# The first phase of a transformer-layer kernel: loads, modulation and stream preparation rewritten in a fixed order

## The chip, the core and the metric

The kernel runs on one core of one Trainium2 chip. The metric is the device time of one execution in microseconds (us). The core's engines are TensorE (PE in the rows; PEld are its weight loads), VectorE (DVE), ScalarE (ACT), GpSimd (POOL) and SyncE (SP, which issues the weight DMAs). The measured time before is the median of three runs; the trace is of one further, profiled execution.

## The reference

One layer works on 256 latent tokens `x` and 256 context tokens `ctx`, each with 2048 channels:

```python
mod   = silu(c) @ w_mod + b_mod          # c: 2048 values; w_mod: 2048 x 12288
mod_c = silu(c_ctx) @ w_mod + b_mod
sa, ca, ga, sm, cm, gm = split(mod, 6)   # the context needs only sa_c, ca_c
h   = rmsnorm(x, nw) * (1 + ca) + sa
h_c = rmsnorm(ctx, nw) * (1 + ca_c) + sa_c
q, k, v from h @ w_in;  k_c, v_c from h_c @ w_in     # rmsnorm over heads, rope on q, k
mix = (sigmoid(g_a) * diff_attention(q, [k, k_c], [v, v_c]) @ w_a_up
     + sigmoid(g_b) * multiscale_pool(h @ w_p) @ w_b_up) @ w_o
x = x + ga * mix
x = x + gm * (relu(modulate(x, sm, cm) @ w_ff1) ** 2 @ w_ff2)
```

The change touches the part up to `h`, `h_c` and the first half of `q` and `k`.

## The kernel before

Every weight is streamed through SBUF in chunks of 512 KB (128 partitions x 1024 floats). `load_next` takes the next chunk of a planned list: SP issues its DMA into one of five `raw` buffers, ACT rounds it to a high half `whi` (L213), DVE subtracts to get the low half `wlo` (L214), and PE multiplies. A product of two floats is made of three products of halves (high x high, high x low, low x high), so a weight chunk of `w_q` or `w_k` with one stream of 256 tokens takes 12 matmuls (L241 to L243), and the chunk of a modulation weight takes four (L347: the two 512-column pieces of `whi` and of `wlo`, against `cv`, whose four columns are the halves of silu(c) and silu(c_ctx)). `whi` and `wlo` have three buffers each; `wchunk` loads two chunks ahead of the one that is used (AHEAD).

The time up to about 167 us is called the first phase here. Its steps in the program are:

- The squares of the x stream are summed (`square_sums`: ACT squares, L459; an add of two tiles, L460; PE sums over partitions with a matrix `mean`, L461) and `rsq` makes the inverse norm `rms[0]` of them.
- `w_m0`, the modulation weights of the first 256 channels, comes in two halves of four chunks, each split like all others.
- Seven stretches m = 1 to 7 follow. Each streams eight chunks of `w_m` (M0 to M7 below) into one PSUM bank, copies the four result rows to SBUF (`mod_rows`, ACT), turns them into columns with four transposes (`mod_columns`, L359, then small DVE operations L365 to L369), and makes with them two of the sixteen 128-channel pieces of the hidden stream of x (`hL`) and of the context (`hC`). `hidden` does that for each piece with a DVE operation that scales and norms (L380), an ACT operation that adds the bias and rounds (L381), and a DVE operation for the low half (L382).
- As soon as pieces exist, `first_steps` multiplies them with the first group of `w_k` for x ("kx"), of the kept `w_k` for the context ("kc"), and of `w_q` ("q"). The split of `w_k` is kept in the tile `first`.
- In stretch 2 the context's squares are summed, with the add of L460 on POOL; its inverse norm is `rms[1]`.

The order in which these instructions stand on each engine's queue is chosen by a scheduler, except for those wrapped in `pin`. The phase's loads all go through SP's queue in the order of the planned list `stream`.

After the phase, `qk_evac` norms and rotates q and k, with the last steps put off by a number of chunks (`later(wait, turn)`), and PE transposes them (`qkT`, L447). `pooling` forms sums over token windows by repeated adds on POOL (L744) and puts off `pool_diff` (edges and differences on DVE, L756 to L760) by three chunks. The two feed-forward products follow: 896 matmuls of 512 and 896 of 256 columns with `w_ff1` as the stationary operand (L939, L942), then `w_ff2`.

Of the kernel before, what the change touches and what calls it, by code (L numbers as in the profile page):

```python
# [17 lines left out]
P = 128  # L18
# [30 lines left out]
def layer(ctx: ExitStack, tc, a, out):  # L49
# [61 lines left out]
    def raw_chunk(src, n=1024):  # L111
        raw = pool.tile([P, n], F32, tag="raw", name="raw", bufs=5)
        nc.sync.dma_start(raw, src)
        return raw
# [9 lines left out]
    def plan(name, *idx, rate=0.0):  # L124
# [8 lines left out]
    for m in range(9):  # L133
        if m == 0:
            for half in range(2):
                for i in range(4):
                    plan("w_m0", half, i)
        for i in range(8 if m > 0 else 0):
            if m < 8:
                plan("w_m", m - 1, i)  # L140
            for at, n, j in carried[m]:
                if at == i and n != "kc":
                    plan("w_k" if n == "kx" else "w_q", 0, j)
            if m == 1 and i > 5 or m == 2 and i < 2:
                plan("cT", (8 * m + i - 14))
            if m == 3 and i == 4:
                plan("prq")
    for n, g, rate in (("w_v", 0, 1.5), ("w_q", 1, 1.0), ("w_k", 1, 1.5), ("w_v", 1, 1.5)):
# [37 lines left out]
    loaded = []  # L186
    done = [0]

    def load_next():
# [14 lines left out]
        raw = raw_chunk(src, n)  # L204
        if key[:2] == ("w_k", 0):
# [17 lines left out]
    def wchunk(*key, ahead=AHEAD):  # L223
        while len(loaded) < min(done[0] + 1 + ahead, len(stream)) or loaded[done[0]][1] is None:
            if loaded and done[0] < len(loaded) and loaded[done[0]][1] is None:
                done[0] += 1
                continue
            load_next()
        got, hi, lo = loaded[done[0]]
        assert got == key, (got, key)  # L230
        loaded[done[0]] = None
# [25 lines left out]

    prm = pool.tile([P, PRM_W], F32, tag="prm", name="prm")
    prq = s8("prq", [P, PRQ_W])
    nc.sync.dma_start(prm, a["prm"])  # L260
    xT = s16("xT", [P, KT, T])
    cT = s16("cT", [P, KT, T])
    for i in range(4):
        nc.sync.dma_start(xT[:, 4 * i:4 * i + 4, :], a["xT"][i])
# [12 lines left out]
    ebias = pool.tile([P, 1], F32, tag="ebias", name="ebias")  # L277
    vec.memset(ebias, -32.0 * math.log(2.0))
    epsb = pool.tile([P, 1], F32, tag="epsb", name="epsb")
# [7 lines left out]
    tc.keep_in_program_order(act.preload_act_table_set("natural_log_exp_and_others"))  # L287
    sil = pool.tile([P, 2, KT], F32, tag="sil", name="sil")
# [6 lines left out]
    b1 = small("b1", 16)  # L295
# [796 lines left out]
```

## Time and profile before

| | us |
|---|---|
| median of three runs | 1522.79 (1521.77 to 1524.62) |
| the profiled execution | 1519.78 |
| its span, first to last instruction | 1517.7 |
| PE busy | 1480.7 (98%) |
| DVE busy | 1063.2 (70%) |
| ACT busy | 755.7 (50%) |
| first DMA queue (weights) | 345.49 MB |

The busy time of PE is a sum of modelled, overlapping matmuls, so a share near 100% does not say that PE runs at its peak. The windows below cut the first phase where the last modulation matmul of a stretch stands: w_m0 ends at 25.8 us, stretch 1 at 43.6, stretch 2 at 72.1, stretch 3 at 89.1, and stretch 7 at 155.2. The profile's mean granted clock of PE is 0.994 of full speed over the span.

### The profile page before, as it was taken

Reading aid. Unit: us, or ns where it says so; the run is one execution under the profiler, and the core shown is the slowest. Engines: PE = TensorE matmul, PEld = TensorE weight load, DVE = VectorE, ACT = ScalarE, POOL = GpSimd, SP = SyncE. Lnnn points to the kernel's source line nnn. Section 1 sums busy time; section 2 is a strip of 40 time slices with the busy share of each in tenths; the row PEclk is TensorE's granted clock in tenths of the full one; section 3 lists DMA queues with packets and bytes.
Section 4 is the critical chain, followed back from the end, with each engine's and each line's share of the span. In section 5 each row is a group of like instructions: output and inputs, shape, how many; then the busy total and the mean of one; then the engine's idle time right before and its main releaser. Section 6 shows DMA issues by size and latency. Waiting matters only on the chain.

```text
span 1517.7 us, 19767 instructions
## 1 busy us (share of the span) xinstructions
PE 1480.7 (98%) x7336; PEld 1232.8 (81%) x7336; DVE 1063.2 (70%) x1280; ACT 755.7 (50%) x1007; POOL 129.3 (9%) x124
## 2 busy tenths in 40 slices
PE   7899999999989999999999999999999999999998
PEld 5677877768878888888879988888888888888887
DVE  7799878777887767666757665666666555555675
ACT  6677534556655444444444554544444454444432
POOL 0100111000140000000000100100000000000170
PEclk9899999999999999999999999999999999999999
DMA  8888668556568787788755677767777666666664
GB/s 314 310 283 308 214 215 285 177 167 193 167 216 300 254 275 272 242 295 296 235 181 168 220 251 245 232 217 244 231 241 240 202 188 193 193 187 193 184 200 142
DMA packets 97439, 347.82 MB, mean 229 GB/s; under 512 B 11072, under 2 KB 11712, under 8 KB 97344
## 3 DMA queue, kind: packets, MB, share of 16 engines
q1 hardware_dynamic: 96768, 345.49, 70.4%
q8 instruction: 57, 0.93, 0.3%
q0 software_dynamic: 576, 1.08, 0.2%
q14 instruction: 38, 0.31, 0.1%
HBM read 344.44 MB, written 2.10 MB: 228 GB/s over the span
## 4 chain that ended last, share of the span: by engine, by line
PE 88%; issue 3%; DVE 3%; DMA 3%; ACT 1%; POOL 1%; DVEq 0%; SPq 0%; ACTq 0%; POOLq 0%
PE f L939 14%; PE f L411 8%; PE f L410 8%; PE f L413 8%; PE f L942 7%; PE pg L413 4%; PE pg L410 4%; PE pg L411 4%; PE pyy L410 2%; PE wo L410 2%; PE wo L413 2%; PE wo L411 2%; PE pyy L413 2%; PE pyy L411 2%; PE v L411 2%
## 5 line engine op out<-in xcount | busy, mean ns | idle before, releaser
L214 DVE TENSOR_TENSOR wlo<-raw,whi 128x1024 fp32r<-128x1024 f32 x507 | 628.6, 1244 | 365.2 <-ACT whi L213 350.9
L213 ACT CAST whi<-raw 128x1024 fp32r<-128x1024 f32 x507 | 529.8, 1047 | 587.3 <-PE f L411 178.1
L939 PE MATMUL f<-h,whi 128*128 128x512 f32 x896 | 224.2, 392 | 0.0
L411 PE MATMUL f<-whi,act 128*128 128x512 f32 x512 | 199.3, 389 | 0.0
L410 PE MATMUL f<-whi,act 128*128 128x512 f32 x512 | 199.3, 389 | 0.0
L939 PEld LDWEIGHTS f<-h,whi 128*128 128x128 f32 x896 | 161.5, 189 | 29.1
L588 DVE SCALAR_TENSOR_TENSOR macc<-raw,sil,macc 128x1024 f32<-128x1024 f32 x128 | 166.2, 1299 | 1.4 <-DMA raw<-in_w_cm_dram 0.8
L413 PE MATMUL f<-wlo,act 128*128 128x512 f32 x512 | 136.8, 389 | 0.0
L942 PEld LDWEIGHTS f<-h,wlo 128*128 128x128 f32 x896 | 122.2, 190 | 8.7
L942 PE MATMUL f<-h,wlo 128*128 128x256 f32 x896 | 124.9, 282 | 0.0
L413 PEld LDWEIGHTS f<-wlo,act 128*128 128x128 f32 x512 | 96.1, 188 | 20.0
L411 PEld LDWEIGHTS f<-whi,act 128*128 128x128 f32 x512 | 96.1, 188 | 19.8
L410 PEld LDWEIGHTS f<-whi,act 128*128 128x128 f32 x512 | 96.1, 188 | 19.8
L410 PE MATMUL pg<-whi,hL 128*128 128x512 f32 x256 | 100.5, 393 | 0.0
L411 PE MATMUL pg<-whi,hL 128*128 128x512 f32 x256 | 99.7, 389 | 0.0
L950 POOL TENSOR_TENSOR rsq<-relu 128x512 f32<-128x512 f32 x28 | 29.2, 1042 | 537.6 <-ACT relu L949 516.7
L413 PE MATMUL pg<-wlo,hL 128*128 128x512 f32 x256 | 68.6, 390 | 2.5 <-DVE wlo L214 2.5
L413 PEld LDWEIGHTS pg<-wlo,hL 128*128 128x128 f32 x256 | 48.0, 188 | 12.9 <-DVE wlo L214 2.9
L410 PEld LDWEIGHTS pg<-whi,hL 128*128 128x128 f32 x256 | 48.1, 188 | 10.1 <-issue 0.2
L411 PEld LDWEIGHTS pg<-whi,hL 128*128 128x128 f32 x256 | 48.1, 188 | 10.1 <-issue 0.2
L410 PE MATMUL wo<-whi,mix 128*128 128x512 f32 x128 | 49.9, 390 | 0.0
L411 PE MATMUL wo<-whi,mix 128*128 128x512 f32 x128 | 49.8, 389 | 0.0
(267 smaller groups left out, 2205.1 us busy)
## 6 DMA issues: line engine op xcount, KB each, us to landing
raw<-in_w_ff_dram SPq DMA_DIRECT2D x240, 512.0 KB, 4.3
raw<-in_w_m_dram SPq DMA_DIRECT2D x64, 512.0 KB, 4.9
raw<-in_w_ga_dram SPq DMA_DIRECT2D x32, 512.0 KB, 4.6
raw<-in_w_cm_dram SPq DMA_DIRECT2D x32, 512.0 KB, 4.6
raw<-in_w_gb_in_dram SPq DMA_DIRECT2D x32, 512.0 KB, 4.5
raw<-in_w_ga_in_dram SPq DMA_DIRECT2D x32, 512.0 KB, 4.4
raw<-in_w_sm_dram SPq DMA_DIRECT2D x32, 512.0 KB, 4.7
raw<-in_w_o_dram SPq DMA_DIRECT2D x32, 512.0 KB, 4.6
```

What stands on the lines that cost most here:

```text
L213: act.copy(hi, raw)
L214: vec.tensor_sub(lo, raw, hi.bitcast(F32))
L410: pe.matmul(banks[t], tok(h, k, 0, tt), wt, start=k == 0, stop=False)
L411: pe.matmul(banks[t], tok(h, k, 1, tt), wt, start=False, stop=False)
L413: pe.matmul(banks[t], tok(h, k, 0, tt), wt, start=False, stop=k == 2 * nk - 1)
L588: pin(vec.scalar_tensor_tensor(acc, raw, sil[:, 0, k:k + 1], acc, ALU.mult, ALU.add))
L939: pe.matmul(ps, hi[:, kk * P:kk * P + P], both(h2, k), start=k == 0, stop=False)
L942: pe.matmul(ps[:, T:2 * T], lo[:, kk * P:kk * P + P], act_slice(h2, k, 0), start=False, stop=k == KT - 1)
L950: gp.tensor_mul(sq, r, r)
```

## The change

All instructions of PE, ACT, DVE and SP in the first phase are now pinned in program order (`ordered_all`), and the program itself is written as a table, `STRETCHES`, of the chunks of each stretch (M: modulation, C: a quarter of the context, K and Q: chunks of `w_k` and `w_q`, T: the rope tables), with a table `then` of what follows each of them. In rows of the changed kernel all such instructions carry line 67, the wrapper's.

- The four chunks of the first half of `w_m0` are loaded ahead of x. `w_m0` is no longer split: PE multiplies the raw floats against `sil`, the two columns silu(c) and silu(c_ctx), with 16 matmuls of 256 columns for each half.
- `hidden` takes streams that were normed before (`scale_stream`, one DVE multiplication for two pieces); ACT scales and adds the bias, rounds both pieces in one cast, and the low half of both is one DVE subtraction, issued behind the next chunk (`low_halves`).
- The context is loaded and squared in stretch 1, and its four adds are on DVE. The chunks of `w_q` come a stretch later than before, so that 60 matmuls of q and k are left behind the last stretch, where there were 48.
- The bias columns are added in one DVE operation instead of two.
- `whi` and `wlo` are placed as six fixed tiles of 1028 floats; the weights that are a stationary operand (`w_p`, `w_ff1a`, `w_ff1`) start 4 floats (16 bytes) into them.
- `qk_evac` waits one chunk longer, `late_split` too, and the `pool_diff` of the last window (g = 3) is put off by five chunks instead of three.

```diff
-            return (lambda *a, **k: pin(emit(*a, **k))) if ordered[0] else emit
-    act, vec = Engine(nc.scalar), Engine(nc.vector)
+            return (lambda *a, **k: pin(emit(*a, **k))) if any(f[0] for f in self.flags) else emit
+    act, vec = Engine(nc.scalar, ordered, ordered_all), Engine(nc.vector, ordered, ordered_all)
+    pe, sp = Engine(nc.tensor, ordered_all), Engine(nc.sync, ordered_all)
...
-    carried = {1: ((1, "kx", 0), (4, "q", 0)), 2: ((2, "kx", 1), (4, "q", 1)),
-               3: ((0, "kc", 0), (3, "kx", 2), (5, "q", 2), (6, "kc", 1))}
+    STRETCHES = [None,
+                 ("M0", "C0", "M1", "C1", "M2", "C2", "K0", "C3", "M3", "M4", "Q0", "M5", "M6", "M7"),
+                 ("M0", "M1", "M2", "M3", "K1", "M4", "M5", "Q1", "M6", "T0", "M7"),
+                 ("M0", "M1", "M2", "M3", "K2", "M4", "M5", "M6", "M7")]
     for m in range(4, 8):
-        carried[m] = ((0, "kc", m - 2), (2, "kx", m - 1), (4, "q", m - 1))
-    carried[8] = ((0, "kc", 6), (0, "kx", 7), (0, "q", 7), (0, "kc", 7))
+        STRETCHES.append(("M0", "M1", f"Q{m - 2}", "M2", "M3", "M4", f"K{m - 1}", "M5", "M6", "M7"))
+    STRETCHES.append(("Q6", "K7", "Q7"))
...
+    STATIONARY, OFFSET = ("w_p", "w_ff1a", "w_ff1"), 4
+    def halves(n, at):
+        i = chunks[0] % 3
+        chunks[0] += 1
+        return [pool.tile([P, 1028], F32R, tag=f"{part}{i}", name=part, bufs=1)[:, at:at + n] for part in ("whi", "wlo")]
...
+        if key[0] == "w_m0":
+            loaded.append((key, raw, raw))
+            return
...
-            hi = pool.tile([P, n], F32R, tag="whi", name="whi", bufs=3)
-            lo = pool.tile([P, n], F32R, tag="wlo", name="wlo", bufs=3)
+            hi, lo = halves(n, OFFSET if key[0] in STATIONARY else 0)
...
+    def mod_whole(half, i, ps, ahead):
+        raw, _ = wchunk("w_m0", half, i, ahead=ahead)
+        for kk in range(4):
+            k = 4 * i + kk
+            pe.matmul(ps[0:2, 0:256], sil[:, :, k], raw[:, kk * 256:kk * 256 + 256], start=k == 0, stop=k == 15)
...
+    def scale_stream(t, k):
+        src = (xT, cT)[t][:, k:k + 2, :]
+        vec.tensor_mul(src, src, rms[t].unsqueeze(1).broadcast_to([P, 2, T]))
...
         for kk in range(n):
-            ht, k8 = h[(k + kk) // 8], (k + kk) % 8
-            u = hw[:, kk, :]
-            bias = c3[:, n + kk, t:t + 1]
-            vec.scalar_tensor_tensor(u, src[:, k + kk, :], c3[:, kk, t:t + 1], rms[t], ALU.mult, ALU.mult)
-            act.activation(ht[:, 0, k8, :], u, AF.Identity, bias=bias)
-            vec.scalar_tensor_tensor(ht[:, 1, k8, :], u, bias, ht[:, 0, k8, :].bitcast(F32), ALU.add, ALU.subtract)
+            act.activation(hw[:, kk, :], src[:, k + kk, :], AF.Identity, bias=c3[:, n + kk, t:t + 1],
+                           scale=c3[:, kk, t:t + 1])
+        hi, lo = ht[:, 0, k8:k8 + n, :], ht[:, 1, k8:k8 + n, :]
+        act.copy(hi, hw)
+        lows.append(lambda: vec.tensor_sub(lo, hw, hi.bitcast(F32)))
...
+    ps = bank("mod")
     for i in range(4):
+        mod_whole(0, i, ps, ahead=3)
+        if i == 0:
+            for q in range(4):
+                sp.dma_start(xT[:, 4 * q:4 * q + 4, :], a["xT"][q])
...
+    for m in range(4, 8):
+        k = 2 * m - 2
+        then[m] = {"M0": [lambda: take_rows(before), partial(context_keys, m - 2), partial(aside, 1)],
+                   "M1": [partial(turn_rows, k), partial(aside, 1)],
+                   "M2": [partial(lambda k: hidden(k, 0, cols[k]), k), partial(aside, 1)],
+                   "M3": [partial(scale_stream, 1, k), partial(aside, 1)],
+                   "M5": [partial(lambda k: hidden(k, 1, cols[k]), k)]}
...
-        qk_evac(kb[t], t, 0, kT, 2, 2 + t)
+        qk_evac(kb[t], t, 0, kT, 2, 3 + t)
...
-            later(3, partial(pool_diff, g, w, ps, sums))
+            later(3 if g < 3 else 5, partial(pool_diff, g, w, ps, sums))
```

The first place is the start of PE's queue (`ssq` is the bank of x's squares, `mod` that of the modulation). Before it read:

```order
L461 MATMUL ssq<-sq,mean 128x256 x8
L347 MATMUL mod<-whi,cv 128x256 x4
L347 MATMUL mod<-wlo,cv 128x256 x4
L347 MATMUL mod<-whi,cv 128x256 x4
L347 MATMUL mod<-wlo,cv 128x256 x4
L347 MATMUL mod<-whi,cv 128x256 x4
```

and in the changed kernel it reads:

```order
L67 MATMUL mod<-raw,sil 2x256 x16
L67 MATMUL ssq<-sq,mean 128x256 x6
L67 MATMUL modT<-prm,rows 128x2 x2
L67 MATMUL ssq<-sq,mean 128x256 x2
L67 MATMUL mod<-raw,sil 2x256 x16
L67 MATMUL mod<-whi,cv 128x512 x2
```

The sums of x's squares moved behind a whole half of w_m0, and 64 matmuls on halves became 32 on raw floats.

The second place is DVE's queue at stretch 2 (`rq_t` and `aT` belong to the inverse norm, `col` to the modulation columns, `hw` to `hidden`). Before:

```order
L365 TENSOR_TENSOR col<-ms 128x8
L367 TENSOR_TENSOR col<-col,b_87 128x4
L369 TENSOR_TENSOR col<-col,prm 128x4
L368 TENSOR_TENSOR col<-col,prm 128x4
L380 SCALAR_TENSOR_TENSOR hw<-xT,col,aT 128x256 x2
L214 TENSOR_TENSOR wlo<-raw,whi 128x1024
L382 SCALAR_TENSOR_TENSOR hL_94<-hw,col,hL_94 128x256 x2
L214 TENSOR_TENSOR wlo<-raw,whi 128x1024
L214 TENSOR_TENSOR first<-raw,first 128x1024
L214 TENSOR_TENSOR wlo<-raw,whi 128x1024 x6
```

and in the changed kernel:

```order
L67 TENSOR_TENSOR wlo<-raw,whi 128x1024 x3
L67 TENSOR_TENSOR col<-ms 128x8
L67 TENSOR_TENSOR col<-col,prm 128x8
L67 TENSOR_TENSOR col<-col,prm 128x4
L67 TENSOR_TENSOR first<-raw,first 128x1024
L67 TENSOR_TENSOR cT<-cT,aT 128x512
L67 TENSOR_TENSOR wlo<-raw,whi 128x1024
L67 TENSOR_TENSOR hL_98<-hw,hL_98 128x512
L67 TENSOR_TENSOR xT<-xT,aT 128x512
L67 TENSOR_TENSOR wlo<-raw,whi 128x1024 x2
```

Four operations of `hidden` on 256 columns became one subtraction and one multiplication on 512, and a subtraction of weights stands between each of them and what it waits for.

The third place is DVE's queue at `pool_diff` of g = 2 (its end, the differences `d` and their low half `dl`) and g = 3 (its start, on the window sums `za` that POOL forms, L758). Before:

```order
L760 SCALAR_TENSOR_TENSOR d<-zb,pin 128x256
L214 TENSOR_TENSOR wlo<-raw,whi 128x1024
L238 TENSOR_TENSOR dl<-d,dh 128x512
L588 SCALAR_TENSOR_TENSOR macc<-raw,sil,macc 128x1024
L238 TENSOR_TENSOR yb<-py,yb 128x512
L758 TENSOR_TENSOR za<-za,prm 128x7 x2
L214 TENSOR_TENSOR wlo<-raw,whi 128x1024
```

and in the changed kernel (its L862 was L758, its L256 was L238):

```order
L864 SCALAR_TENSOR_TENSOR d<-zb,pin 128x256
L256 TENSOR_TENSOR dl<-d,dh 128x512
L692 SCALAR_TENSOR_TENSOR macc<-raw,sil,macc 128x1024
L231 TENSOR_TENSOR wlo<-raw,whi 128x1024
L256 TENSOR_TENSOR yb<-py,yb 128x512
L862 TENSOR_TENSOR za<-za,prm 128x7 x2
L231 TENSOR_TENSOR wlo<-raw,whi 128x1024
```

The two short multiplications stay ahead of the same subtraction of weights; one other subtraction moved from ahead of `dl` to behind it.

## Rows read from the trace of the kernel before

**Rows 1.** The page's busy times: busy us, share of the span, instructions.

```profile
PE 1480.7 (98%) x7336; PEld 1232.8 (81%) x7336; DVE 1063.2 (70%) x1280; ACT 755.7 (50%) x1007; POOL 129.3 (9%) x124
```

**Rows 2.** Windows: length, busy PE, PEld, DVE, ACT, POOL; clock, DMA share, GB/s.

```profile
0.00:25.80 25.80, 15.83 (x83) 12.60 (x84) 17.28 (x31) 18.20 (x26) 1.82 (x6) 1.00 0.90 317
25.80:43.60 17.80, 15.26 (x59) 9.69 (x57) 12.82 (x16) 9.90 (x12) 0.00 (x0) 1.00 0.92 342
43.60:72.10 28.50, 25.09 (x90) 18.04 (x90) 23.86 (x28) 21.64 (x31) 7.23 (x4) 0.82 0.82 281
72.10:89.10 17.00, 17.00 (x77) 13.48 (x75) 16.61 (x34) 12.03 (x17) 0.00 (x0) 1.00 0.81 262
...
155.20:171.00 15.80, 15.17 (x70) 12.26 (x69) 11.85 (x27) 9.24 (x16) 0.42 (x1) 1.00 0.60 228
```

**Rows 3.** Windows: stretches 4 to 7 together, the fastest loads, the slow clock.

```profile
89.10:155.20 66.10, 65.05 (x285) 50.47 (x285) 60.72 (x99) 47.90 (x63) 0.00 (x0) 1.00 0.87 304
...
38.00:43.00 5.00, 3.81 (x15) 2.03 (x14) 2.45 (x2) 2.04 (x2) 0.00 (x0) 1.00 1.03 416
43.00:53.00 10.00, 7.46 (x19) 3.93 (x19) 6.83 (x11) 7.66 (x13) 2.80 (x2) 0.62 0.91 347
```

**Rows 4.** DVE groups by shape, 0 to 171 us: busy us, mean ns, idle before.

```profile
L214 DVE TENSOR_TENSOR wlo<-raw,whi 128x1024 fp32r<-128x1024 f32 x75 | 93.1, 1259 | 16.9 <-ACT whi L213 16.4
L382 DVE SCALAR_TENSOR_TENSOR hL<-hw,col,hL 128x256 fp32r<-128x256 f32 x16 | 8.1, 541 | 0.0
L380 DVE SCALAR_TENSOR_TENSOR hw<-cT,col,aT 128x256 f32<-128x256 f32 x16 | 7.2, 476 | 0.0
L460 DVE TENSOR_TENSOR sq<-sq 128x512 f32<-128x512 f32 x4 | 2.8, 692 | 4.3 <-ACT sq L459 4.3
L318 DVE TENSOR_TENSOR tabs<-prq 128x32 f32<-128x32 f32 x8 | 1.1, 183 | 0.0
```

**Rows 5.** ACT groups by shape, 0 to 171 us, same columns.

```profile
L213 ACT CAST whi<-raw 128x1024 fp32r<-128x1024 f32 x75 | 77.7, 1047 | 29.2 <-DVE wlo L214 8.4 <-DMA raw<-in_w_m_dram 7.3 <-PE mod L347 5.8
L381 ACT ACTIVATE hL<-hw,col 128x256 fp32r<-128x256 f32 x16 | 7.4, 502 | 6.4 <-DVE hw L380 6.2
L459 ACT ACTIVATE sq<-cT 128x512 f32<-128x512 f32 x8 | 4.7, 622 | 0.0
```

**Rows 6.** Timeline of PE in the first feed-forward product: start, length, count.

```profile
1115.77 1.98 PE L939 MATMUL f<-h,whi 128*128 128x512 f32 x8
1117.58 1.12 PE L942 MATMUL f<-h,wlo 128*128 128x256 f32 x8
1118.53 2.00 PE L939 MATMUL f<-h,whi 128*128 128x512 f32 x8
1120.37 0.40 PE L942 MATMUL f<-h,wlo 128*128 128x256 f32 x2
```

**Rows 7.** Timeline at the start and in stretch 2: plain-float matmuls, x's first piece.

```profile
58.43 1.02 PE L461 MATMUL ssq<-sq,mean 128*128 128x256 f32 x4
59.10 0.58 PE L241 MATMUL w_k<-first,hL 128*128 128x512 f32 x1
...
5.75 1.15 ACT L459 ACTIVATE sq<-xT 128x512 f32<-128x512 f32 x2 [0.96 <-DMA xT<-in_xT_dram]
```

**Rows 8.** Timeline of stretch 2: DVE's subtractions beside POOL's adds.

```profile
54.85 6.80 DVE L214 TENSOR_TENSOR wlo<-raw,whi 128x1024 fp32r<-128x1024 f32 x4
...
53.87 4.43 POOL L460 TENSOR_TENSOR sq<-sq 128x512 f32<-128x512 f32 x2 [1.16 <-DVE wlo L214]
```

**Rows 9.** PE's waits, 171 to 500 us: total us, times, longest.

```profile
PE qkT L447 <- POOL qm L440: 3.0, 2, 2.0
PE pg L413 <- DVE wlo L214: 2.5, 1, 2.5
```

**Rows 10.** Timeline of DVE and POOL at `pool_diff` of g = 3.

```profile
444.45 0.17 DVE L758 TENSOR_TENSOR za<-za,prm 128x7 f32<-128x7 f32 x1 [2.87 <-POOL za L744]
...
436.27 1.64 POOL L744 TENSOR_TENSOR zb<-za 128x271 f32<-128x271 f32 x1 [6.96 <-DVE dl L238]
```

More of the change, by code (lines that the diff above doesn't have):

```diff
@@ L338, in tok, with mod_chunk @@
         return tiles[k // 8][:, part, k % 8, t * P:t * P + P]
-    def mod_chunk(key, i, ps, n):
-        hi, lo = wchunk(*key, i)
-        per = 1024 // n
+    def mod_chunk(m, i, ps):
+        hi, lo = wchunk("w_m", m - 1, i)
         for part in (hi, lo):
-            for kk in range(per):
-                k = per * i + kk
-                pe.matmul(ps[:, 0:n], cv[:, k, :], part[:, kk * n:kk * n + n], start=(k == 0 and part is hi),
+            for kk in range(2):
+                k = 2 * i + kk
+                pe.matmul(ps, cv[:, k, :], part[:, kk * 512:kk * 512 + 512], start=(k == 0 and part is hi),
@@ L483, in first_steps @@
                 yield
-    def steps(g, n):
-        for _ in range(n):
-            next(g, None)
-    sb = bank("ssq")
-    for i in range(4):
-        square_sums(xT, vec, sb, i)()
-    rms = [rsq(sb[:, 0:T], T, P / D, "aT")]
-    cols = {}
-    for half in range(2):
-        ps = bank("mod")
-        for i in range(4):
-            mod_chunk(("w_m0", half), i, ps, 256)
-            if half == 1 and i == 1:
-                cols[0] = mod_columns(0, rows, 1)
-                hidden(0, 0, cols[0], 1)
-        rows = mod_rows(ps, 256)
@@ L533, in layer, with context_keys, aside, turn_rows @@
-    c3 = mod_columns(14, rows)
-    hidden(14, 0, c3)
-    hidden(14, 1, c3)
-    for _, n, j in carried[8]:
-        steps(first_steps(n, j), 4)
+    side = []
+    def context_keys(j):
+        side.append(first_steps("kc", j))
+    def aside(n):
+        while side and n:
+            if next(side[0], True):
+                side.pop(0)
+            else:
+                n -= 1
+    rms = [None, None]
+    cols = {}
+    rows = [None]
+    sums = []
+    sb = bank("ssq")
+    def turn_rows(k, n=2, r=4):
+        cols[k] = mod_columns(k, rows[0], n, r)
@@ new lines, in take_rows, with norms, squares @@
+    def take_rows(ps, r=4, n=512):
+        rows[0] = mod_rows(ps, r, n)
+    def norms(t):
+        rms[t] = rsq(sb[:, 0:T], T, P / D, "aT")
+    def squares(i):
+        while sums:
+            sums.pop(0)()
+        if i < 4:
+            sums.append(square_sums(cT, vec, sb, i))
+    ps = bank("mod")
+    for i in range(4):
+        mod_whole(0, i, ps, ahead=3)
+        if i == 0:
+            for q in range(4):
+                sp.dma_start(xT[:, 4 * q:4 * q + 4, :], a["xT"][q])
+    for i in range(4):
+        if i == 3:
+            take_rows(ps, 2, 256)
+        summed = square_sums(xT, vec, sb, i)
+        if i == 3:
+            turn_rows(0, 1, 2)
+        summed()
@@ new lines, in layer @@
+    norms(0)
+    ps = bank("mod")
+    for i in range(4):
+        mod_whole(1, i, ps, ahead=1)
+        if i == 0:
+            scale_stream(0, 0)
+            hidden(0, 0, cols[0], 1)
+            scale_stream(0, 2)
+            low_halves()
+        else:
+            scale_stream(0, 2 + 2 * i)
+    sb = bank("ssq")
+    then = {m: {} for m in range(1, 9)}
+    then[1] = {"M0": [lambda: take_rows(before, 2, 256)], "M1": [partial(turn_rows, 1, 1, 2)],
+               "M2": [lambda: hidden(1, 0, cols[1], 1)], "K0": [partial(squares, 0)], "M3": [partial(squares, 1)],
+               "M4": [partial(squares, 2)], "Q0": [partial(squares, 3)], "M5": [partial(squares, 4)],
+               "M6": [partial(norms, 1)]}
@@ new lines, in layer @@
+    for m in range(1, 8):
+        before, ps = ps, bank("mod")
+        for step in STRETCHES[m]:
+            kind, i = step[0], int(step[1])
+            if kind == "M":
+                mod_chunk(m, i, ps)
+            elif kind in "KQ":
+                for _ in first_steps("kx" if kind == "K" else "q", i):
+                    pass
+            low_halves()
+            for f in then[m].get(step, ()):
+                f()
+    last = first_steps("q", 6)
+    context_keys(6)
+    next(last)
@@ L538, in layer @@
+    take_rows(ps)
+    next(last)
+    turn_rows(14)
+    for _ in last:
+        pass
+    hidden(14, 0, cols[14])
+    low_halves()
+    aside(4)
+    hidden(14, 1, cols[14])
+    low_halves()
+    for n, j in (("kx", 7), ("q", 7), ("kc", 7)):
+        for _ in first_steps(n, j):
+            pass
+    ordered_all[0] = False
     kb, qb = fb["w_k"], fb["w_q"]
@@ L581, in late_gen @@
                         o = dst[:, half * 1024:half * 1024 + 1024]
[L582 removed]
+                        later(3 if credit_rate[0] < 1 else 2, partial(late_split, acc, norm_w, o))
                         parts.append(waiting[-1])
```

155 lines of the change are left out of this document (74 added, 81 removed).

## The prediction

> **What bounds the kernel now.** I read the page first: PE is busy for 98% of the span [rows 1], and that number has to be taken apart before it says anything, because matmuls overlap in it. In the first feed-forward product eight matmuls of 512 columns take 1.81 us from start to start and eight of 256 columns 0.95 us, so 0.226 and 0.119 us each [rows 6]. Then I cut the first phase into windows by stretch and set the matmuls in them against that pace. A stretch from 4 to 7 owes 32 modulation matmuls and 36 of q and k: 68 x 0.226 = 15.4 us, with transposes 15.8. The four took 66.1 us, 16.5 each, with DVE busy for 60.7 and ACT for 47.9 of it [rows 3]. These are near to what PE needs. Stretch 2 is not: it took 28.5 us for hardly more than 60 such matmuls, its granted clock was 0.82, and the loads ran at 0.82 of their share [rows 2]. In the ten microseconds from 43 us the clock stood at 0.62, between its two levels of 1.2 and 2.4 GHz, behind a stretch in which PE was busy for 3.81 us of 5 [rows 3]. In the same stretch POOL adds the context's squares, two in 4.43 us, and four subtractions beside them took 6.80 us, 1.70 each [rows 8], where the mean over the phase is 1.26 [rows 4]. Stretch 1 runs at 342 GB/s with a DMA share of 0.92 [rows 2]: the loads limit it. After the phase PE waits little: 3.0 us for the rotated keys and queries and once 2.5 us for a subtraction [rows 9]. So what can be won sits in stretch 2, some in the handovers of the other stretches, and a few microseconds in the late waits.
>
> **The end of the phase before.** The last stretch's modulation ends at 155.2 us and the window up to 171.0 holds 70 matmuls [rows 2]; 16 of these belong to v already (3.6 us), so the phase's own work ends at about 15.8 - 3.6 behind 155.2, at 167.4 us.
>
> **Start and w_m0.** A load of 512 KB costs, by 342 GB/s over a share of 0.92, 524.3 KB / 372 = 1.41 us; the bounds are 1.53 (342 as it stands) and 1.26 (416 GB/s at 38 us) [rows 2, 3]. The first piece of x was there at 5.75 us [rows 7]; now the first w_m0 chunk is. The four chunks of half 0 are there by 10.0, x by 15.6. A plain-float matmul of 256 columns is two records; four records run from 58.43 to 59.10 at the least and 1.02 long as modelled [rows 7], so 0.34 to 0.51 each, and I take 0.44: 16 make 7.0 us. Half 0 lies below the wait for x. The last square of x then costs 1.15 (two ACT squares [rows 7]), 0.69 (the add [rows 4]) and 0.9 on PE: 18.3. Half 1 follows with 7.0: 25.3, where w_m0 ended at 25.8 [rows 2]. Eight casts and eight subtractions are gone (8 x 1.05 on ACT, 8 x 1.26 on DVE [rows 4, 5]), but PE's work grew and x comes 5.6 us later: I count nothing.
>
> **Stretch 1.** The four context loads came into it, so its last chunk is load 26 of the phase: 5.75 + 25 x 1.41 = 41.0, then cast 1.05, subtraction 1.23, two matmuls 0.45: 43.7. I take 44.6, one worse than 43.6, because all four queues are now in one order and ACT has eight squares in it (8 x 0.62 [rows 5]); bounds 40 (1.26) and 46.7 (1.53).
>
> **Stretch 2.** PE has 62 matmuls and four transposes: 14.5 us. DVE has ten subtractions; without the four slow ones these cost (75 x 1.259 - 6.80) / 71 = 1.23 [rows 4, 8]. To them come the column operations (three of 0.18), four scalings and three low halves. The nearest row for a 128x512 scaling is the add of squares at 0.69, and for a low half twice the old ones, 0.95 [rows 4]; I take 0.69 for four scalings and 0.5 each for the low halves, of which two are of 256 columns, and a little over 1 for what is left of the norm. In all 12.3 + 0.5 + 2.8 + 1.5 + 0.7 = 17.8 us. The adds of squares are no longer here (they are four times 0.69 in stretch 1, below its loads). DVE sets the stretch: 28.5 becomes 17.8, -10.7.
>
> **Stretch 3** has nine subtractions (11.1), the rope tables (some 17 operations of about 0.18 [rows 4], 3.0) and 2.6 of scalings and low halves: 16.7 against 17.0 [rows 2].
>
> **Stretches 4 to 7.** For each chunk pair `hidden` cost DVE four operations of 0.48 to 0.54 for one stream [rows 4]; now it is one of 0.69 and one of at most 0.69. DVE: 10 x 1.23 + 4 x 0.69 + 0.5 = 15.6. ACT gains a cast: 10 x 1.05 + 4 x 0.50 + 2 x 0.62, and two short copies below 0.62 each [rows 5], 14.9. Loads: 10 x 1.41 = 14.1. PE's 15.8 is the longest, and I add 0.6 for handovers: 16.4 each, 65.6 against 66.1 [rows 3]. The old order left more in the air at 155.2 us; what is left behind stretch 7 now is 60 matmuls instead of 48, 13.6 with transposes and a short wait 14.2, against 12.2.
>
> The sum is 44.6 + 17.8 + 16.7 + 65.6 + 14.2 = 158.9, **-8.5 us**. If PE never waits after stretch 1 the same sum is 44.6 + 14.5 + 15.4 + 63.2 + 13.6 = 151.3, -16; if the handovers cost 1.3 per stretch and stretch 1 ends at 46.7 it is 167, nothing.
>
> **Behind the phase.** The transposes of q and k come one chunk later; a chunk of v is 24 matmuls, 5.4 us, longer than the longest wait of 2.0 [rows 9]: **-3.0** (0 to -3.0). The delay of `pool_diff` for g = 3 does less than its number says: the multiplications that DVE waited at (L758, 2.87 us the second time [rows 10]) are not pinned and still stand ahead of the same subtraction. But POOL's adds wait for the low half of g = 2 [rows 10], and one subtraction (1.23) moved behind that, so they start that much earlier: **-1.2** of PE's 2.5 (0 to -2.5). The longer delay of `late_split` is covered: DVE is busy for 70% [rows 1] and nothing on PE asks for that result soon. If the cover fails it costs one such operation, below 1.3.
>
> **The shift of 16 bytes.** No row shows weights at another address. The 256-column matmuls take 0.119 us where half of 0.226 is 0.113, and eight of 512 behind them take 1.84 (1118.53 to 1120.37) instead of 1.81 [rows 6]: 896 x 0.006 + 112 x 0.03 = 8.7 us is the most that a faster weight load could give, and I let a slower one cost as much. I take 0, since the gap is 2 to 5% and may have another cause. The Trainium skill, in "TensorE: Matmul & The Clock Gate", Step-by-step: what each phase is for, says that the array has two independent SBUF read ports, so that loading the next weights takes nothing from the moving operand; by that rule the shift gives nothing, and the sum is the same. No run here shows it; the 0.03 us by which a run of 512 columns starts slower behind one of 256 is what speaks against it.
>
> **The sum.** -8.5 - 3.0 - 1.2 = -12.7 against the profiled execution's 1519.8: 1507.1. That execution lies 3.0 under the median of the three runs (1522.8), to which the forecast is set: **1510 us**. A measurement of this kernel can tell about 0.2%, 3 us, from no change.
>
> **Rivals.**
> *Slower: the fixed order chains ACT and DVE.* Every cast, copy and square now stands in one row on ACT, and a subtraction of DVE behind a scaling that waits for ACT holds up all later weights. DVE waits for the cast 16.4 us in the phase already [rows 4]. In stretches 1 to 7 the old order passed 70 chunks (56 of the modulation, seven each of k and q) in 129.4 us, 1.85 a chunk; my sum passes 69 from 25.3 to 144.7, 1.73. Fully serial, a cast and a subtraction are 1.05 + 1.23 = 2.28. It decides at 1.91 a chunk (12.7 / 69 = 0.18 above my sum), where the phase's gain and the late 4.2 are gone; at 2.0 the phase is 69 x 0.27 = 18.6 longer than summed, 1529. Against it: two chunks are loaded ahead and low halves stand behind the next subtraction. Chance 0.12.
> *The phase gains little.* Stretch 1 feeds PE only at the pace of the loads, the clock falls again, and ten microseconds at half level take 5 us of PE: stretch 1 ends at 46.7, stretch 2 takes 20, stretch 3 17.0, the four 66.1, the rest 14.2: 164, -3.4; with the late waits moved elsewhere or gone, 1515.5 to 1521.5. For it: the clock did fall behind stretch 1 [rows 3]. Against: stretch 2 has 3 us of slack on PE. Chance 0.20, half of it within 0.2%.
> *Near PE's own pace, or the shift pays.* PE waits nowhere after stretch 1, or the feed-forward products gain some of the 8.7: 1490 to 1502. Chance 0.16.
>
> **The numbers.** My forecast, 1502 to 1515.5, has 0.52. The range leaves out the slow rival's upper part and the lowest corner: 1495 to 1522. Faster 0.78 (0.52 + 0.16 + 0.10), same 0.10, slower 0.12.
>
> **What would show it.** Right: stretch 2 near 18 us at a clock near 1.00, modulation ended near 145 us, the last matmul of k at about 159, subtractions at 1.23 throughout, no wait of PE for the rotated queries, a feed-forward pace unchanged at 0.226 and 0.119. Wrong: casts of ACT that wait for PE or DVE more than before, the clock below 1.00 in stretches 1 or 2, stretches 4 to 7 at 17 or more, or a changed spacing in the products with shifted weights.

## The result and the profile after

The changed kernel took 1529.56 us (median of five runs, 1528.95 to 1530.89) against 1522.66 for the kernel before, a ratio of 1.005 with a 95% interval of 1.0035 to 1.0065. It is 0.5% slower, where 1510 was forecast. The profiled execution took 1528.95 us with a span of 1527.1, 9.4 longer than the span before.

The page's busy line of the changed kernel answers to [rows 1]: PE has 6.9 us more, DVE 15.7 less.

```profile
PE 1487.6 (97%) x7336; PEld 1232.8 (81%) x7336; DVE 1047.5 (69%) x1235; ACT 758.8 (50%) x1017; POOL 121.8 (8%) x120
```

The windows of the changed kernel are cut at w_m0, the seven stretches (five to seven of them together as 110.9 to 164.5) and the rest; the columns are those of [rows 2]:

```profile
0.00:25.80 25.80, 20.67 (x82) 8.95 (x82) 10.68 (x24) 11.92 (x20) 1.82 (x6) 1.00 0.90 335
25.80:49.20 23.40, 20.84 (x75) 14.79 (x74) 16.46 (x20) 15.92 (x25) 0.00 (x0) 0.85 0.88 315
49.20:69.50 20.30, 16.39 (x64) 12.26 (x63) 15.88 (x22) 14.58 (x21) 0.00 (x0) 0.92 0.82 272
69.50:87.00 17.50, 15.57 (x70) 12.37 (x69) 12.50 (x16) 13.77 (x19) 0.00 (x0) 1.00 0.83 271
87.00:110.90 23.90, 19.93 (x74) 14.87 (x73) 16.95 (x36) 14.03 (x20) 0.00 (x0) 0.86 0.63 196
110.90:164.50 53.60, 50.43 (x218) 38.47 (x217) 43.12 (x51) 41.60 (x55) 0.00 (x0) 1.00 0.88 293
164.50:180.50 16.00, 14.67 (x67) 11.62 (x66) 10.19 (x16) 10.71 (x19) 0.00 (x0) 1.00 0.68 235
```

Three of the stretches have a granted clock below 1.00, where before it was one [rows 2]; no engine is full in any of them. The first phase ends at 180.3 us, 13.1 later than before.

One correction to the reading of before: [rows 2] were cut at the column transposes (L359), and in the kernel before these stand some chunks behind the modulation matmul that ends a stretch; the window called stretch 2 there holds 45 modulation matmuls, not 32. Counted by matmuls (32 to a stretch), its stretches 2 and 3 took 23.8 and 20.4 us, not 28.5 and 17.0, so stretch 2 had less to win than forecast and stretch 3 more. The table counts all kernels so, from the starts of matmuls in the traces, us; the phase's end is the last matmul of k or q less 0.227 for each matmul of v that went ahead of it. The lower rows belong to experiments that are told below.

| kernel | w_m0 ends | s1 | s2 | s3 | s4 | s5 | s6 | s7 | rest | phase ends |
|---|---|---|---|---|---|---|---|---|---|---|
| before | 25.6 | 17.7 | 23.8 | 20.4 | 16.9 | 17.0 | 17.1 | 16.4 | 12.1 | 167.1 |
| forecast | 25.3 | 19.3 | 17.8 | 16.7 | 16.4 | 16.4 | 16.4 | 16.4 | 14.2 | 158.9 |
| changed | 25.8 | 23.5 | 20.3 | 17.5 | 23.9 | 18.1 | 18.1 | 17.5 | 15.8 | 180.3 |
| no_shift | 25.6 | 23.1 | 21.4 | 19.1 | 23.6 | 18.1 | 18.1 | 17.4 | 15.4 | 181.9 |
| unpinned | 24.7 | 25.5 | 19.1 | 15.3 | 16.2 | 16.9 | 16.4 | 16.0 | 14.4 | 164.6 |
| pe_free | 25.0 | 22.2 | 17.2 | 15.6 | 19.1 | 19.4 | 18.7 | 17.4 | 14.7 | 169.3 |
| act_dve_free | 24.7 | 25.4 | 22.6 | 20.4 | 16.7 | 16.6 | 16.2 | 16.7 | 14.4 | 173.8 |
| unpinned_ctx_later | 25.5 | 22.8 | 19.0 | 15.3 | 16.0 | 17.3 | 16.2 | 16.4 | 14.2 | 162.6 |

*no_shift* has the same first phase as the changed kernel, and its trace ends the phase 1.6 us later: a stretch or a phase end read from one trace carries about that much scatter.

PE's waits of the changed kernel in the first phase (total us, times, longest) name what it stood for; the 5.1 us are the wait for the first load, at the start:

```profile
PE modT L67 <- ACT rows L67: 6.1, 3, 3.2
PE mod L67 <- DMA raw<-in_w_m_dram: 5.1, 1, 5.1
PE w_k L67 <- DVE hL L67: 4.0, 2, 2.1
PE w_k L67 <- DVE first L67: 3.2, 5, 0.7
PE mod L67 <- DVE wlo L67: 1.4, 4, 0.4
PE w_k L67 <- ACT hL L67: 1.4, 1, 1.4
```

The timeline shows two of these places. In stretch 2 the chunk K1 stands at the head of PE's line (PE rows); at stretch 4 the exponential of the rope tables stands at the head of ACT's (ACT row), and PE's transposes behind it:

```profile
55.91 0.73 PE L67 MATMUL w_k<-first,hL 128*128 128x512 f32 x2 [1.41 <-ACT hL L67]
58.72 4.15 PE L67 MATMUL w_k<-first,hL 128*128 128x512 f32 x10 [2.08 <-DVE hL L67]
...
91.88 0.20 ACT L67 ACTIVATE lam<-lam 128x2 f32<-128x2 f32 x1 [4.36 <-DVE lam L67]
...
93.55 0.59 PE L67 MATMUL modT<-prm,rows 4*128 4x4 f32 x4 [3.19 <-ACT rows L67]
94.07 1.65 PE L67 MATMUL w_k<-first,hC 128*128 128x512 f32 x3
```

Windows around the second place show what the pause is followed by:

```profile
89.00:93.00 4.00, 1.36 (x6) 0.59 (x4) 3.09 (x20) 1.12 (x3) 0.00 (x0) 0.99 0.75 236
93.00:95.00 2.00, 1.45 (x6) 1.33 (x7) 1.75 (x2) 2.00 (x5) 0.00 (x0) 0.50 0.09 35
95.00:100.00 5.00, 5.00 (x14) 3.82 (x13) 2.28 (x5) 0.46 (x1) 0.00 (x0) 0.53 0.81 249
```

PE was busy for 1.36 us of 4, and then the clock stood at its lower level of 1.2 GHz: three matmuls of 512 columns took 1.45 us from start to start instead of 0.68. The exponential waits 4.4 us for the last of a row of small DVE operations, and stretch 4 is 7.0 us longer than before (23.9 against 16.9).

### The profile page after: what moved, and what is told of

It reads as the page before. It is cut to its first block, busy times and chain, and to the rows that moved or that the text cites. A ratio compares the mean times of both kernels' runs of the same rounds, so it can differ in the third digit from the quotient of the medians.

```text
span 1527.1 us, 19692 instructions
## 1 busy us (share of the span) xinstructions
PE 1487.6 (97%) x7336; PEld 1232.8 (81%) x7336; DVE 1047.5 (69%) x1235; ACT 758.8 (50%) x1017; POOL 121.8 (8%) x120
## 4 chain that ended last, share of the span: by engine, by line
PE 89%; DVE 4%; ACT 3%; issue 2%; DMA 1%; POOL 1%; DVEq 0%; SPq 0%; POOLq 0%; ACTq 0%
PE f L1043 13%; PE f L452 8%; PE f L451 8%; PE f L454 8%; PE f L1046 7%; PE pg L454 4%; PE pg L451 4%; PE pg L452 4%; PE mod L67 3%; PE w_k L67 2%; PE pyy L451 2%; PE wo L451 2%; PE wo L454 2%; PE pyy L452 2%; PE wo L452 2%; PE pyy L454 2%
## 5 line engine op out<-in xcount | busy, mean ns | idle before, releaser
L231 DVE TENSOR_TENSOR wlo<-raw,whi 128x1024 fp32r<-128x1024 f32 x433 | 537.5, 1243 | 349.8 <-ACT whi L230 338.2
L230 ACT CAST whi<-raw 128x1024 fp32r<-128x1024 f32 x433 | 453.6, 1049 | 565.6 <-PE f L452 178.1
L67 DVE TENSOR_TENSOR wlo<-raw,whi 128x1024 fp32r<-128x1024 f32 x67 | 80.5, 1222 | 25.8 <-ACT whi L67 25.6
L67 ACT CAST whi<-raw 128x1024 fp32r<-128x1024 f32 x67 | 68.6, 1047 | 32.9 <-PE w_q L67 12.0
```

The source lines that it names most:

```text
L67: return (lambda *a, **k: pin(emit(*a, **k))) if any(f[0] for f in self.flags) else emit
L230: act.copy(hi, raw)
L231: vec.tensor_sub(lo, raw, hi.bitcast(F32))
```

## The experiments

Each ratio is to runs of the kernel before beside it; an interval of 95% stands in brackets.

**The order.** Four kernels change only what is pinned; three of them stand here, the fourth (*unpinned_edges*) under the late waits. *unpinned* drops the two lines that switch `ordered_all`; *pe_free* and *act_dve_free* free one side:

```diff
-    ordered_all[0] = True
...
-    ordered_all[0] = False
...
-    pe, sp = Engine(nc.tensor, ordered_all), Engine(nc.sync, ordered_all)
+    pe, sp = nc.tensor, Engine(nc.sync, ordered_all)
...
-    act, vec = Engine(nc.scalar, ordered, ordered_all), Engine(nc.vector, ordered, ordered_all)
+    act, vec = Engine(nc.scalar, ordered), Engine(nc.vector, ordered)
```

> The changed kernel with the same program text, but its first phase not pinned: the scheduler orders PE, ACT, DVE and SP again. Theory (order): the phase of the changed kernel ends 12.8 us later because PE, ACT and DVE wait in a fixed line behind late instructions; without the pins 8 to 13 us come back, 1517 to 1521 us, ratio to before 0.996 to 0.999. Rival (work): the unsplit w_m0 and the four loads moved into stretch 1 cost the time whatever the order; the ratio stays at 1.004 to 1.006.

Measured: 0.9966 [0.9954, 0.9979]. The phase ends at 164.6 us, 15.7 earlier than pinned, with the same instructions on every engine. The order is the cause, and without the pins the change is a gain.

> The changed kernel with PE alone left to the scheduler in the first phase; ACT, DVE and SP stay in program order. Theory A (PE's own line is what waits: a matmul that is not ready holds up others that are, and the clock falls behind the longer pauses): most of the unpinned kernel's gain appears, phase end at 168 to 172 us, ratio to before 0.998 to 1.001. Theory B (ACT's and DVE's lines are late, PE only shows it): phase end at 177 or later, ratio 1.003 to 1.005.

> The changed kernel with ACT and DVE left to the scheduler in the first phase; PE and SP stay in program order. Theory A: phase end at 173 to 178 us, only the 5 us of the held-up exponential come back, ratio 1.001 to 1.003. Theory B: phase end at 166 to 170 us, ratio 0.997 to 0.999.

Measured: pe_free 0.9985 [0.9976, 0.9994], phase end 169.3; act_dve_free 1.0015 [1.0007, 1.0024], phase end 173.8. Freeing PE's line gives 11.0 us of the 15.7 and freeing ACT's and DVE's 6.5 (SP stays pinned in both), as theory A had it. The stretches tell more than these sums. With PE free, stretches 1 to 3 take 55.0 us instead of 61.3, and stretches 4 to 7 take 74.6 instead of 77.5. With ACT and DVE free, stretches 4 to 7 take 66.2, almost as unpinned (65.6), but stretches 1 to 3 take 68.4. So ACT's and DVE's lines cost 11.3 us in the late stretches, far more than the exponential, and their freedom costs 7.1 in the early ones, where PE still stands in line for pieces of the hidden stream: the row of act_dve_free comes first, then the one of pe_free (PE's waits in the phase):

```profile
PE w_k L67 <- ACT hL L422: 7.6, 2, 4.2
```

```profile
PE w_k L259 <- ACT hL L67: 1.5, 1, 1.5
```

**Two repairs inside the fixed order.** *tables_apart* issues the exponential behind M4 of stretch 4:

```diff
-        act.activation(lam2, lam2, AF.Exp)
+        lams.append(lam2)
...
+        if m == 4:
+            then[m]["M4"] = [lam_exp]
+            then[m]["M5"].append(lam_end)
```

> The changed kernel with the exponential of the rope tables (ACT) issued five chunks behind the small DVE operations that it waits for, and the two DVE operations behind it later still. Theory (ACT held up at the head of its line for 4.4 us, then PE for 3.2 us and at the lower clock): stretch 4 falls from 23.9 us to 18 or 19 and the time by 4 to 6, ratio 1.001 to 1.003. Rival (the tables' 3 us of DVE work are what costs): stretch 4 stays above 22 and the time falls by at most 2.

Measured: 1.0034 [1.0022, 1.0047]; stretch 4 falls from 23.9 to 19.4 us and the phase's end from 180.3 to 175.3, nearly as far as the theory had it, and well past the rival. The interval of the ratio overlaps that of the changed kernel, so the 5 us are shown by the trace.

*keys_later* moves K1 and K2 two chunks down, and the first matmuls of the context's keys from behind Q1 to behind K1:

```diff
-                 ("M0", "M1", "M2", "M3", "K1", "M4", "M5", "Q1", "M6", "T0", "M7")
+                 ("M0", "M1", "M2", "M3", "M4", "M5", "K1", "M6", "Q1", "T0", "M7")
-                 ("M0", "M1", "M2", "M3", "K2", "M4", "M5", "M6", "M7")
+                 ("M0", "M1", "M2", "M3", "M4", "M5", "K2", "M6", "M7")
```

> The changed kernel, all pinned, with the chunk of w_k two steps later in stretches 2 and 3 (behind M5 instead of M3), so that it stands further behind the pieces of the hidden stream that it multiplies. Theory (PE stands at the head of its line for the low half of the hidden stream, 4.0 us in two waits, and once the clock falls behind it): stretches 2 and 3 fall from 20.3 and 17.5 to 18 and 16, ratio 1.002 to 1.004. Rival (DVE is late as a whole, and the wait moves to the next chunk): both stretches keep their length, ratio 1.004 to 1.006.

Measured: 1.003 [1.0019, 1.004], but not for the reason given. Stretches 2 and 3 together took 37.2 us instead of 37.8, which is within the scatter: the waits moved to the next chunks, as the rival had it. The trace shows the gain in stretch 4 (21.6 instead of 23.9), where the pause before the transposes is 2.57 instead of 3.19 us.

**The start.** *wm0_split* gives w_m0 back its casts and subtractions (matmuls on `whi`, `wlo` against `cv`); *unpinned_ctx_later* and *tables_apart_ctx_later* move the context's loads down:

```diff
-                 ("M0", "C0", "M1", "C1", "M2", "C2", "K0", "C3", "M3", "M4", "Q0", "M5", "M6", "M7"),
+                 ("M0", "M1", "M2", "C0", "K0", "C1", "M3", "C2", "M4", "C3", "Q0", "M5", "M6", "M7"),
```

> The changed kernel with w_m0 split into halves again (64 matmuls of 256 columns on halves, eight casts and subtractions), all else as changed. Theory (the raw buffers of w_m0 are held until PE has used them, so later loads stall): w_m0 and stretch 1 together end 2 to 4 us earlier, ratio 1.002 to 1.004. Rival (the casts and subtractions that come back cost more): no change or up to 3 us longer.

Measured: 1.0107 [1.0092, 1.0123]; my theory fell, and the loss is larger than the rival's 3 us. w_m0 ends at 34.5 us instead of 25.8, stretch 1 is 3.6 shorter, the phase ends 6.4 later. In this order the unsplit w_m0 is a gain.

> The unpinned kernel with the four loads of the context two or three places later in stretch 1 (behind M2, K0, M3, M4), so that M2 and K0 load ahead of them; their squares stay where they were. Theory (in the unpinned kernel, too, PE pauses 3.0 us for M2, whose load stands behind two context loads and the buffers of w_m0, and the clock falls to half level behind it): the pause is below 1 us, the clock stays up, stretch 1 falls from 25.5 us to 20 or 22, the time by 3 to 5, ratio to before 0.993 to 0.995. Rival (the buffers of w_m0 alone hold the load up): ratio 0.996 to 0.997.

> The kernel with the exponential apart, all pinned, with the context's loads at the same later places. Theory (a fixed order is good where its lines are not held up): stretch 1 falls by 3 to 5 us as well, ratio to before 1.000 to 1.002. Rival (with all in one line the pause moves to the next late instruction): ratio 1.003 to 1.004.

Measured: 0.9926 [0.9914, 0.9939], the fastest version found, against 0.9966 for *unpinned*; and 1.0039 [1.0027, 1.0052] under pins, no gain. PE's pause in stretch 1, in the unpinned kernel and then with the loads moved:

```profile
31.63 1.01 PE L366 MATMUL mod<-whi,cv 128*128 128x512 f32 x2 [2.96 <-ACT whi L230]
```

```profile
32.28 0.74 PE L259 MATMUL w_k<-first,hL 128*128 128x512 f32 x2 [1.11 <-ACT first L230]
```

Stretch 1 falls from 25.5 to 22.8, less than expected: the clock still falls, from the window 30 to 35 us on (0.85 and 0.81 in 35 to 40, where the unpinned kernel has 0.69 and 0.63). The two ratios are about 6 us apart; of these the traces show 2.0 in the phase and about as much at `pool_diff`, where PE waits 1.9 us instead of 3.3, and the rest is not placed. Under pins the same moves gave nothing in the phase: stretch 1 took 24.6 us, where *tables_apart* has 23.5. Stretch 3 took 19.1 instead of 17.5, but so it did in *no_shift*, whose loads were not moved.

**The shift and the placed tiles.** *no_shift* is the changed kernel with OFFSET = 0. *before_shift* brings `halves` (tiles of 1028 floats) and the shift into the kernel before, *before_shift_turns* the later transposes too. *before_placed* lays the tiles out as the changed kernel does, the small tiles included, with shift 0, *before_placed_shift* with 16 bytes. *unpinned_rotating* is unpinned_ctx_later with the old rotating buffers and no shift.

```diff
-    STATIONARY, OFFSET = ("w_p", "w_ff1a", "w_ff1"), 4
+    STATIONARY, OFFSET = ("w_p", "w_ff1a", "w_ff1"), 0
```

> The changed kernel with the stationary weights at the same place as all others (shift 0 instead of 16 bytes). Theory (the shift pays): the feed-forward products, 4.1 us shorter than before, go back, and the time is 3 to 5 us longer, ratio 1.007 to 1.008, with eight 512-column matmuls behind a 256-column run at 1.84 us again. Rival (the 4.1 us have another cause, or the shift does nothing): no change.

Measured: 1.0087 [1.0073, 1.0101]. From the first matmul of the feed-forward products to the last it takes 713.5 us without the shift, 709.6 with it (713.6 before). Of the 112 runs of eight 512-column matmuls that follow 256-column ones, 106 are 1.84 us long from start to start without the shift, as the second in [rows 6] (1118.53 to 1120.37), and 111 are 1.81 with it, as here (1129.92 to 1131.73):

```profile
1129.92 1.98 PE L1043 MATMUL f<-h,whi 128*128 128x512 f32 x8
1131.73 1.11 PE L1046 MATMUL f<-h,wlo 128*128 128x256 f32 x8
```

> The kernel before with the six placed tiles and the shift of 16 bytes for the three stationary weights, and nothing else. Theory (the shift pays by itself): the feed-forward products 4.1 us shorter, ratio 0.997 to 0.998. Rival (it pays only beside other parts of the change, or placing the tiles by hand costs something): ratio 0.999 or above.

> The kernel before with the shift and with the transposes of q and k one chunk later. Theory (the delay takes PE's 3.0 us of waits at the rotated queries): 2 to 3 us less than the kernel with the shift alone, ratio 0.995 to 0.9965. Rival (the wait moves to another wait of attention): ratio as with the shift alone.

Measured: 1.0173 [1.0159, 1.0187] and 1.0176 [1.0163, 1.019], 26 us slower: the rivals' side, but far beyond what they had in mind. Five of the six tiles stood at other addresses (32 and 96 for the high halves, 0, 64 and 128 for the low ones, modulo 256 bytes, as the program was built, instead of 224), and all matmuls with a weight chunk as the moving operand slowed. The mean spacing of matmul starts, ns, from the traces:

```
                             before   before_shift   before_placed
f<-whi,act  512 columns       226.9      230.6          226.9
f<-wlo,act  512 columns       226.7      233.2          226.7
pg<-wlo,hL  512 columns       227.4      233.6          226.7
f<-h,whi    512 columns       230.4      232.7          230.4
```

Taken tile by tile, the same two `f` groups of before_shift differ within one run: 228.6, 230.3 and 233.0 ns for the high halves at 224, 32 and 96, and 234.1, 233.1 and 232.3 for the low halves at 0, 64 and 128. The tile that stayed at 224 is slower than before too, so the place modulo 256 bytes is not the whole rule.

> The kernel before with the split weights in six fixed tiles, laid out as in the changed kernel (every tile at the same address modulo 256 bytes as before), shift 0. Theory P (addresses: in the kernel before_shift the tiles of 1028 floats stood at other residues, which slowed PE, and the layout itself is innocent): ratio 0.998 to 1.002. Rival Q (fixed tiles, one of three in turn, hold the scheduler's order up): ratio 1.005 or more, with longer stretches in the first phase.

> As before_placed, with the shift of 16 bytes for the three stationary weights. Theory (the shift pays by itself, 4.1 us in the feed-forward products): 0.0027 below the ratio of before_placed. Rival (it does not): the same ratio.

> The kernel unpinned_ctx_later with three rotating buffers each for the split weights, as before the change, at the same residue, and without the shift. Theory P: 4.1 us longer for the missing shift and nothing else, ratio to before 0.995 to 0.9965. Rival Q (fixed tiles hold up the order here as well): the first phase is shorter than 163 us and the ratio 0.993 or less.

Measured: before_placed 1.006 [1.0046, 1.0074], before_placed_shift 1.0037 [1.0023, 1.005], unpinned_rotating 0.9942 [0.993, 0.9954]. With the addresses right the spacing is that of before, so rival Q holds for the kernel before: six fixed tiles make its phase 12.3 us longer (179.4 instead of 167.1). *before_shift*, which leaves the small tiles as they were, ends it at 180.4, of which its slower matmuls are an estimated 1.6 us (320 of them by some 5 ns, from the table), so the layout of the small tiles is not what does it. In the changed program the fixed tiles cost little: with rotating buffers its phase ends at 161.8 instead of 162.6, and the ratio, which lies between the theory and the rival, is 0.0016 higher for the shift that is missing. One cost is the same in both programs: ahead of the feed-forward products PE waits 5.2 us for `yt` in the kernels with six fixed tiles and 4.2 in those with rotating buffers. Here are the changed kernel and unpinned_rotating:

```profile
PE h2T L985 <- DVE yt L67: 5.2, 1, 5.2
```

```profile
PE h2T L980 <- DVE yt L67: 4.2, 1, 4.2
```

The shift by itself gives 0.0023 in the kernel before. Without it the feed-forward products take 713.3 to 714.4 us in five kernels, with it 709.2 to 711.3 in eleven (before_shift and before_shift_turns, with their other addresses, left out).

**The late waits.** *before_turns* only delays the transposes (`3 + t`, `7 + t`); *unpinned_edges* pins the second multiplication of `pool_diff`.

> The kernel before with the transposes of q and k one chunk later, nothing else. Theory (PE's 3.0 us of waits at the rotated queries go): ratio 0.998, the wait gone from PE's list. Rival (the wait moves on): ratio 0.9995 or above.

> The unpinned kernel with the two short multiplications of pool_diff pinned behind their pinned neighbours, so that the two subtractions of weights go ahead of them. Theory (DVE stands there for POOL's sums 2.5 and 2.9 us, PE then 2.5 to 3.3): the wait is gone, 2 to 4 us less than the unpinned kernel, ratio to before 0.994 to 0.996. Rival (POOL's sums are late and the wait comes back at the differences): ratio as unpinned, 0.996 to 0.997.

Measured: before_turns 0.9976 [0.9968, 0.9985], and no wait for the rotated queries is left. unpinned_edges 0.9961 [0.9949, 0.9972], as unpinned: DVE lets the subtractions through, and PE waits for POOL a few matmuls later, in this row of its timeline:

```profile
442.39 2.00 PE L787 MATMUL osum<-osq,mean 128*128 128x512 f32 x2 [2.48 <-POOL osq L783]
```

## Why the prediction was wrong

**The step that failed is the sum of the stretches.** The phase ended 21.4 us later than summed (180.3 against 158.9); what stands behind it came out within 0.5 of its forecast in total, and that by luck, as the shift's gain and the loss at `pool_diff`, both missed, cancel. The sum took for each stretch the longest engine and added 0.6 us for handovers. That is about how long the stretches take when every engine does whatever is ready: unpinned, stretches 2 to 7 took 100.0 us in all, against 100.1 summed, though luck has a part in that, as stretch 2 is 1.3 longer than summed and stretch 3 1.4 shorter. Pinned, they took 115.3. I noted which instructions move, but counted none of the waits that a fixed line adds. Subtractions stayed at 1.22 us, and the longer ones beside POOL's adds [rows 8] are gone, so DVE's work fell as forecast.

The slower rival, at a chance of 0.12, came nearest: it named the fixed order, and its pace of 2.0 us a chunk (1529) is what came, 138.7 us for 69 chunks. It put the waits on ACT and DVE. That is true of the late stretches; in the first three it is PE's own line that costs, where a matmul that waits for a piece of the hidden stream holds up modulation chunks that are ready. The lines also hold up each other. ACT's casts of `whi` waited for PE to release a tile for 21.4 us in the changed kernel's phase, as the first two rows have it, and for 8.4 before:

```profile
ACT whi L67 <- PE w_q L67: 12.0, 6, 5.0
ACT whi L67 <- PE mod L67: 9.4, 7, 3.5
```

```profile
ACT whi L213 <- PE mod L347: 5.8, 7, 2.1
ACT whi L213 <- PE w_q L242: 1.5, 1, 1.5
ACT whi L213 <- PE w_q L243: 1.1, 1, 1.1
```

**Stretch 1** was mis-sized in every version: it ends at 49.2 pinned and 50.2 unpinned, where 44.6 was forecast. Over its whole window the loads have room (share 0.88), but at its start they do not: from 25 to 35 us their share is 0.91 and 1.02, and ACT stands 3.0 us for the load of M2. PE pauses behind that, and the clock is at its lower level while K0's twelve matmuls run. Moving two of the context's loads behind M2 gave 2.7 us of it in the unpinned kernel.

```profile
28.92 1.04 ACT L67 CAST whi<-raw 128x1024 fp32r<-128x1024 f32 x1 [3.01 <-DMA raw<-in_w_m_dram]
```

**The low clock multiplies a pause.** I gave it to one rival and to stretch 1. The changed kernel has it at four places: behind the pauses in stretch 1, 1.41 and 2.08 us in stretch 2, 3.19 in stretch 4, and 3.29 at `pool_diff`. But the length of a pause does not settle whether it follows. Behind the same wait in stretch 3, ten matmuls took 2.56 us in the changed kernel and 4.15 in no_shift; that difference of 1.6 us is as much as the two phase ends are apart:

```profile
79.86 2.56 PE L67 MATMUL w_k<-first,hL 128*128 128x512 f32 x10 [1.93 <-DVE hL L67]
```

```profile
80.51 4.15 PE L67 MATMUL w_k<-first,hL 128*128 128x512 f32 x10 [1.92 <-DVE hL L67]
```

**pool_diff (-1.2)** failed. The step was that POOL's adds wait for the low half of g = 2. That was done earlier, but the first add also needs ACT's copy of `za`, which now stands behind a weight cast of 1.05 us that was done earlier in the kernel before; counted from the first score matmul, POOL started 0.9 us later than before, DVE's two waits are 2.53 and 2.87 us as before, and PE waited 3.29 us instead of 2.48. The clock, which had stayed at 1.00 before, then fell to 0.50 in the next 5 us:

```profile
446.41 1.47 POOL L848 TENSOR_TENSOR zb<-za 128x271 f32<-128x271 f32 x1 [7.91 <-ACT za L844]
...
455.80 2.08 PE L454 MATMUL pg<-wlo,hL 128*128 128x512 f32 x4 [3.29 <-DVE wlo L231]
...
454.41 0.17 DVE L862 TENSOR_TENSOR za<-za,prm 128x7 f32<-128x7 f32 x1 [2.87 <-POOL za L848]
...
455.00:460.00 5.00, 4.20 (x8) 2.69 (x9) 4.97 (x7) 0.48 (x1) 0.12 (x1) 0.50 0.61 186
```

From the first score matmul to the first of w_o the changed kernel is 3.2 us longer (451.1 against 447.9). The part of the clock in it is not the same in every run: behind an unchanged pause at this place the kernel before kept its pace, and before_turns did not (four matmuls in the first and the second row):

```profile
445.84 1.20 PE L413 MATMUL pg<-wlo,hL 128*128 128x512 f32 x4 [2.48 <-DVE wlo L214]
```

```profile
440.86 1.84 PE L413 MATMUL pg<-wlo,hL 128*128 128x512 f32 x4 [2.46 <-DVE wlo L214]
```

**The transposes (-3.0)** were right: 3.4 us shorter from the phase's end to the second group of q (50.1 to 46.7), and 0.9976 by themselves.

**The shift (0)** was wrong in size: -4.0, inside the bound of 8.7 and near the 112 x 0.03 worked out from [rows 6]. The Trainium skill says in "TensorE: Matmul & The Clock Gate", Step-by-step: what each phase is for, that loading the next weights takes nothing from the moving operand; by that rule the shift would have given nothing. The measurement does not go with it: moving the stationary weights by 16 bytes alone took the spacing from 230.4 to 226.6 ns. How the place of the weights slows a matmul is not shown.

**w_m0 (nothing)** was right against before (25.8 and 25.6), but by two errors that cancel: the 8.7 us by which wm0_split ends it later show a gain of the unsplit w_m0, and the new order of the start took as much; how much of that is x's later arrival, no run shows.

The terms close: +13.1 (phase) - 3.4 (transposes) - 0.5 (up to the first scores) + 3.2 (pool_diff and its surroundings) + 0.9 (the wait for `yt`) - 4.0 (shift) is, but for rounding, +9.4, the difference of the spans.

Open: why six fixed tiles cost the kernel before 12.3 us of its phase and the changed program little; why the clock falls behind some pauses and not behind others of the same length; of the 4.2 us by which stretches 5 to 7 are longer than unpinned (53.6 against 49.4), which go back when ACT and DVE are free (49.5), what each of the two is worth; and how much of stretch 1 a better order of loads could still win.

## What to carry to other kernels

A sum of engine work per stage gives the time of a stage only where nothing stands in line; before an order is written out by hand, read for each instruction at the head of a queue what it waits for and what ready work stands behind it. Change the parts one at a time: here the same program without the pins was 0.9966, and 0.9926 with the context's loads moved down as well, while the whole change as made was 1.005. Look at each stage for which engine's line costs: freeing ACT and DVE won 11 us in one half of the phase and lost 7 in the other. A pause of PE can cost its own length and slow matmuls after it: a 4.4 us wait of ScalarE became a PE pause of 3.2 us and came to about 5 us at the phase's end.

## What the runs showed of the hardware that was not expected

- Where operands stand in SBUF sets the pace of 512-column matmuls. With the weights as the moving operand, tiles all at 224 modulo 256 bytes ran 226.7 to 226.9 ns apart; in before_shift a tile at 32 ran at 230.3, one at 96 at 233.0, and those at 0, 64 and 128 at 234.1 to 232.3, and the one left at 224 at 228.6. With the weights stationary and the other operand read in two pieces of 256, it was 230.4 ns with both at 224 and 226.6 with the weights 16 bytes on.
- The length of a pause of PE does not tell what the clock does behind it. Pauses of 3.19 and 3.29 us were each followed by 5 to 7 us at a granted clock of 0.50 to 0.53; at one place of the program a pause of 2.48 us was followed by 5 us at 1.00 (before) and one of 2.46 by 5 us at 0.66 (before_turns).
